# Last layer of a four-layer backbone: the high and low halves of 256 tokens read as one moving operand of 512 columns

## The chip, the core and the metric

The kernel runs on one core of a Trainium2 chip. TensorE (PE) multiplies, VectorE (DVE) and ScalarE (ACT) do the elementwise work, GpSimd (POOL) issues a few DMAs, SyncE (SP) issues most of them. The metric is the device time of one execution in microseconds; lower is better. Each engine works through its own queue in the order in which the program put it there, and waits at the head of the queue when an operand is not ready.

## What is computed

A latent stream of 256 tokens and a context stream of 256 tokens, each 1024 wide, pass through four layers. Each layer is a mixer and a squared-ReLU MLP, each ahead of it a normalisation with shift and scale, behind it a gated residual. In the last layer the context stream is not needed any more beyond the mixer's keys and values, so its output projection and its MLP run on 256 tokens only.

```python
def sq_relu_mlp(x, w1, w2):
    return jnp.square(jax.nn.relu(x @ w1)) @ w2
...
    h = h + ml[2][:, None] * yl
    xl = modulate(rmsnorm(h, norm_g[l, 1]), ml[3][:, None], ml[4][:, None])
    h = h + ml[5][:, None] * sq_relu_mlp(xl, mlp_w1[l], mlp_w2[l])
```

Here `x` is (256, 1024), `w1` is (1024, 4096), `w2` is (4096, 1024), all float32. The output is the latent stream after a last normalisation.

## The kernel before

Every large product is made in three matmuls, because operands are split into a rounded high part (type fp32r) and the rest, a low part: high weight by high data, high weight by low data, low weight by high data (`mm3`, L388 to L392). Data lie transposed: 128 features on the partitions, tokens along the free axis, so that `xh` and `xl` hold for each of 8 feature chunks the 512 token columns, latent tokens in columns 0 to 255 (`LT`), context tokens behind them (`CT`).

A *chunk* is one packed weight tile of 128 x 1024: 8 blocks of 128 x 128, one for each step k over 1024 inputs. `chunk` (L404) fetches the weights, takes the next of six PSUM banks, issues 8 x 3 matmuls into it and then the evacuation of the bank. In layers 0 to 2 a matmul has 512 moving columns; in the last layer's output projection (L799) and MLP (L692 to L699) it has 256.

The order of the work around a chunk is that of the code, with nothing moved by a scheduler. `w_get` (L266) stands ahead of a chunk's matmuls and with `ahead=4` splits the weights that will be used four chunks later: ACT casts them to the high part `whi` (L241), DVE subtracts to get the low part `wlo` (L246), and then the DMA of another raw tile is issued. There are five pairs of `whi` and `wlo`, so the cast of a new one waits until PE has finished the chunk ahead of the present one. Behind the matmuls of the chunk come its evacuation's instructions, so that on ACT and DVE alike the order is: split for chunk m+4, evacuation of chunk m, split for chunk m+5, evacuation of chunk m+1, and so on.

The MLP runs in four blocks of hidden features. In each, a first half of 8 chunks makes 8 x 128 hidden features from `xh`, `xl` (evacuation `ev1`, L668), and a second half of 8 chunks multiplies these by `w2` and adds the result to `h` (`residual`, L558). The evacuation of a first-half chunk is on ACT: `r` = relu of the bank (L673), `hh` = its square rounded (L674), `q` = its square (L675); and on DVE `hl` = `q` - `hh` (L676). Step k of every chunk in the second half reads `hh`, `hl` of hidden chunk k, so the first chunk of the second half comes at its last step to the hidden chunk that was evacuated last. The evacuation of a second-half chunk is one DVE instruction (L565): `h` = bank x gate + `h`. The first three hidden chunks of an MLP are made inside `transition` (L577), behind the normalisation, and go through `ev1` too.

After the last block of the MLP, and in the last output projection, `stats_late` (L436) adds squares of `h` for the next normalisation.

Of the kernel before, what the change touches and what calls it, by code (L numbers as in the profile page):

```python
# [8 lines left out]
F32 = mybir.dt.float32  # L9
F32R = mybir.dt.float32r  # L10
# [3 lines left out]
ALU = mybir.AluOpType  # L14
# [8 lines left out]
NK = 8  # L23
# [10 lines left out]
HID_RING = 10  # L34
# [95 lines left out]
def ada_order():  # L130

    return [(l, cc) for l in range(DEPTH) for cc in range(0 if l else PE_ADA, 48)]
# [71 lines left out]
CT, LT, ALL = slice(T, 2 * T), slice(0, T), slice(0, 2 * T)  # L204
# [3 lines left out]
class Body:  # L208
# [185 lines left out]
    def unit(self, out, w, xk, sl, ks=range(NK)):  # L394

        for k in ks:
            hi, lo = xk(k)
            c = slice(k * 128, k * 128 + 128)
            self.mm3(out, w[0][:, c], w[1][:, c], hi[:, sl], lo[:, sl], k == 0, k == NK - 1)

    def x_chunk(self, k):
        return self.xh[:, k, :], self.xl[:, k, :]

# [154 lines left out]
    def residual(self, l, gate, stats):  # L558
# [14 lines left out]

        return evac


    def transition(self, tail, norm, n_head, evac_head, both):  # L577

# [82 lines left out]
    def mlp(self, l, last):  # L661
        nc = self.nc
        full = LT if last else ALL
        with ExitStack() as st:
            p1 = self.block_pool(st, f"mlp{l}", "right")
            hid = [(p1.tile([128, 512], F32R, name=f"hh{j}"), p1.tile([128, 512], F32R, name=f"hl{j}")) for j in range(4)]

            def ev1(ci, o, sl):  # L668
                n = sl.stop - sl.start
                hh, hl = hid[ci % HID_RING]  # L670
                r = p1.tile([128, 512], F32, tag="r", name="r", bufs=2)
                q = p1.tile([128, 512], F32, tag="q", name="q", bufs=1)
                nc.scalar.activation(r[:, :n], o, AF.Relu)  # L673
                nc.scalar.activation(hh[:, sl], r[:, :n], AF.Square)  # L674
                nc.scalar.activation(q[:, :n], r[:, :n], AF.Square)  # L675
                nc.vector.tensor_tensor(out=hl[:, sl], in0=q[:, :n], in1=hh[:, sl].bitcast(F32), op=ALU.subtract)  # L676

            yield 3, ev1
            p2 = self.block_pool(st, f"mlpb{l}", "right")
            hid += [(p2.tile([128, 512], F32R, name=f"hh{j}"), p2.tile([128, 512], F32R, name=f"hl{j}")) for j in range(4, HID_RING)]  # L680
            step = [0]
            if not last:
                p3_ctx = self.tc.tile_pool(name=f"mlpc{l}", bufs=1, side="right", reuse_waits="tile")
                p3 = p3_ctx.__enter__()
                self.conditions(p3)

            def pump():
                step[0] += 1
                if not last and step[0] > 2:
                    self.ada_pump(2 if step[0] % 6 else 1, l + 1)  # L690

            for b in range(4):  # L692
                for m in range(3 if b == 0 else 0, 8):
                    self.chunk(b * 8 + m, self.x_chunk, full, ev1)
                    pump()
                src = lambda k, b=b: hid[(b * 8 + k) % HID_RING]
                res = self.residual(l, 40, full.stop if b == 3 else 0)
                for m in range(5 if b == 3 and not last else 8):
                    self.chunk(m, src, full, res)  # L699
                    if b < 3 or m < 3:  # L700
                        pump()
            if not last:
                p3_ctx.__exit__(None, None, None)
            yield None if last else (src, res, (5, 6, 7))


    def mixer_a(self, l, i, last):
        nc, tc = self.nc, self.tc
        full = LT if last else ALL
        n = full.stop  # L710
        units = mixer_a_units()
        with ExitStack() as st:
# [38 lines left out]
            for u in range(n_head, len(units)):  # L751
                if units[u][0] == "gate":
                    w = self.w_get()
                    o = self.bank()
# [16 lines left out]
            for nh in range(2):  # L771
                outs = [self.bank() for _ in range(4)]
                for kk in range(4):
                    w = self.w_get()
# [11 lines left out]
                for tcn in range(4):  # L786
                    dst = vx[:, tcn, nh * 4 : nh * 4 + 4, 0:128]
                    src = outs[tcn].rearrange("p (h v) -> p h v", h=4)
# [8 lines left out]
            self.scan(l, i, last, sp, lp or sp, dnm, dar, qT, kT, vx, tok, saved, n)  # L797
        res = self.residual(l, 16, n)
        for m in range(3, 8 if last else 5):  # L799
            self.chunk(m, self.x_chunk, full, res, ahead=2 if last else 4)  # L800
        yield None if last else (self.x_chunk, res, (5, 6, 7))

    def gates(self, rows, dr, i, gps, last):
# [838 lines left out]
    def run(self):  # L1642
        nc = self.nc
        self.order = weight_order()
        self.ada_list = ada_order()
        self.n_ada = PE_ADA + len(self.ada_list)
        self.lows = []
        self.raw, self.hl, self.ada_raw, self.mods, self.rs, self.cur = {}, {}, {}, {}, {}, {}
        self.wpos = self.wsplit = self.apos = self.bpos = self.xpos = 0
        nc.scalar.preload_act_table_set("natural_log_exp_and_others")  # L1650
        cst = self.pool("cst", 1)
        big = self.pool("big", 1)
        self.modp = self.pool("mod", 2)
        self.nrm = self.pool("nrm", 1)
        self.adap = self.pool("ada", N_ADA)
        self.rawp = self.pool("raw", N_RAW)
        self.hlp = self.pool("hl", N_HL)
        self.dram = self.pool("dram", 1, space=DRAM)
        psum = self.pool("psum", 1, space=PSUM)
        self.allb = psum.tile([128, 8, 512], F32, name="bank")  # L1660
        self.banks = [self.allb[:, j, :] for j in range(8)]

        self.vecs = cst.tile([128, NV], F32, name="vecs")
        cons = self.cons = cst.tile([128, NC], F32, name="cons")
        self.cs = cst.tile([128, 8, 32], F32, name="cs")
        self.hgn = cst.tile([128, 16], F32, name="hgn")
        sk = cst.tile([128, 16], F32, name="sk")
        nc.sync.dma_start(out=self.vecs, in_=self.vecs_in)
        self.held = None
        self.sel = cst.tile([128, 2], F32, name="sel")  # L1670
        nc.gpsimd.dma_start(out=self.sel, in_=self.consts_in[:, CC["sel"] : CC["sel"] + 2])
        self.h = big.tile([128, 8, 512], F32, name="h")
        self.xh = big.tile([128, 8, 512], F32R, name="xh")
        self.xl = big.tile([128, 8, 512], F32R, name="xl")
        self.sq = cst.tile([128, 512], F32, name="sq")
        self.ssum = cst.tile([128, 512], F32, name="ssum")

        def con(name, w, rows=128):
            return cons[0:rows, CC[name] : CC[name] + w]

        self.ident, self.rot = con("ident", 128), con("rot", 128)
        self.cos, self.sin = con("cos", T), con("sin", T)
        self.mask_f, self.mask_b = con("mask_f", 128), con("mask_b", 128)
        self.ones = cst.tile([128, 128], F32, name="ones")
        nc.vector.memset(self.ones, 1.0)
        self.ones_row = self.ones
        self.eps = cst.tile([128, 1], F32, name="eps")
        nc.vector.memset(self.eps, EPS)
        nc.gpsimd.dma_start(out=sk, in_=self.sinks_in.to_broadcast([128, 16]))
        self.nsinks = cst.tile([128, 16], F32, name="nsinks")  # L1690
        self.ident16 = cst.tile([128, 128], BF16, name="ident16")
        self.mask_w = cst.tile([128, 2 * T], BF16, name="mask_w")

        def mixer(l):
            kind, i = l % 3, l // 3
            if kind == 0:
                return self.mixer_a(l, i, l == DEPTH - 1)
            return self.mixer_b(l, i) if kind == 1 else self.mixer_c(l, i)

        prev = mixer(0)  # L1700
        _, evac = next(prev)
        self.start(5, evac)
        nc.vector.tensor_scalar(self.hgn, self.vecs[:, VC["a_head_g"] : VC["a_head_g"] + 16], -1.0, None, op0=ALU.mult)
        nc.vector.tensor_scalar(self.nsinks, sk, -1.0, None, op0=ALU.mult)
        tail = prev.send(5)
        for b in range(1, 2 * DEPTH):
            l, which = divmod(b, 2)
            block = self.mlp(l, l == DEPTH - 1) if which else mixer(l)
            n_head, evac = next(block)
            self.transition(tail, (l, which), n_head, evac, tail is not None)  # L1710
            next(prev, None)
            prev = block
            tail = next(block)
        step = self.rstd_begin(0, self.stats_mm(0, more=self.sq_late))
        for c in range(NK - 2, NK):
            self.scale_out(c)
        step()
        for c in range(0, NK, 2):
            hc = self.h[:, c : c + 2, LT]
            self.nc.vector.tensor_tensor(out=hc, in0=hc, in1=self.rs[0].unsqueeze(1).to_broadcast([128, 2, T]), op=ALU.mult)  # L1720
            (self.nc.sync, self.nc.scalar)[c // 2 % 2].dma_start(out=self.out[:, c : c + 2, :], in_=hc)
        next(prev, None)
# [29 lines left out]
```

## Time and profile before

| | us |
|---|---|
| median of 3 runs | 2112.53 (2112.12 to 2112.61) |
| profiled execution, its own time | 2114.74 |
| its span, from first to last instruction | 2113.0 |
| PE busy | 2053.4 (97%) |
| DVE busy | 1453.5 (69%) |
| ACT busy | 948.9 (45%) |
| last layer's MLP, first chunk behind `transition` to its last matmul | 1925.34 to 2101.2 |

A row of a timeline gives the start, the duration, the engine, the line of the kernel, the operation, its operands and, in brackets, how long the engine was idle before it and what released it. The end of a matmul is modelled, since matmuls are pipelined; the distance between the starts of two of them is what one costs. The granted clock of TensorE (`PEclk`) is 1.00 at 2.4 GHz and 0.50 at 1.2 GHz; a value between is a stretch that holds both.

### The profile page before, as it was taken

To read this page: it belongs to the slowest core of one execution; us is meant where nothing else is said; L and a number is where in the kernel's file an instruction comes from. 1 tells how busy PE (TensorE), PEld (TensorE's weight loads), DVE (VectorE), ACT (ScalarE), POOL (GpSimd) and SP (SyncE) were. 2 spreads that over 40 slices of the span, in tenths; PEclk is the share of its full clock that TensorE was granted. 3 is DMA by queue.
4 is the path that set the end of the run, shared out by engine and by line. 5 is a ranking of instruction groups with operands and counts; after the bars stand their busy time and mean duration, and the time that the engine had idled before them with its cause. 6 is when DMAs were issued, how large, how long until landed. Compare 5 with 4: busy or idle time off the path is not lost.

```text
span 2113.0 us, 30325 instructions
## 1 busy us (share of the span) xinstructions
PE 2053.4 (97%) x11730; PEld 1751.2 (83%) x11730; DVE 1453.5 (69%) x2652; ACT 948.9 (45%) x1814; POOL 87.0 (4%) x138
## 2 busy tenths in 40 slices
PE   6989999999999999999999999999999999989998
PEld 4767798888889878988888988898888899889997
DVE  5667777787777775677777764467777776576554
ACT  3436653324236685624333343262433435556554
POOL 0123100000000000000000000000000000310000
PEclk9999999999999999999999999999999999999999
DMA  9783245565553104266565433236556533635552
GB/s 300 272 264 103 64 135 179 177 193 185 184 170 119 50 2 138 92 189 189 179 194 175 130 112 98 94 108 189 187 180 197 179 122 104 175 103 180 184 185 91
DMA packets 97025, 326.11 MB, mean 154 GB/s; under 512 B 17760, under 2 KB 18928, under 8 KB 96240
## 3 DMA queue, kind: packets, MB, share of 16 engines
q1 hardware_dynamic: 81184, 293.81, 43.5%
q0 software_dynamic: 15152, 29.83, 4.6%
q8 instruction: 92, 1.51, 0.3%
q10 hardware_dynamic: 544, 0.52, 0.1%
q14 instruction: 53, 0.43, 0.1%
HBM read 319.73 MB, written 4.33 MB: 153 GB/s over the span
## 4 chain that ended last, share of the span: by engine, by line
PE 92%; DVE 3%; DMA 2%; ACT 2%; issue 1%; POOL 0%; SPq 0%; DVEq 0%; ACTq 0%
PE bank L390 25%; PE bank L392 25%; PE bank L391 25%; PE bank L591 2%; PE bank L592 2%; PE bank L594 2%; PE bank L422 1%; PE bank L1348 1%; PE bank L423 1%; PE bank L424 1%; PE bank L1360 1%; DMA ab<-dar 1%; PE bank L1288 1%; PE bank L1025 1%; DVE wlo L246 1%; PE bank L1000 1%
## 5 line engine op out<-in xcount | busy, mean ns | idle before, releaser
L390 PE MATMUL bank<-xh,whi 128*128 128x512 f32 (+1 forms) x1600 | 579.4, 362 | 1.7 <-ACT h L912 1.0
L241 ACT CAST whi<-raw 128x1024 fp32r<-128x1024 f32 x374 | 387.1, 1044 | 421.1 <-PE bank L391 382.8
L391 PE MATMUL bank<-xl,whi 128*128 128x512 f32 (+1 forms) x1600 | 574.4, 359 | 0.2
L392 PE MATMUL bank<-xh,wlo 128*128 128x512 f32 (+1 forms) x1600 | 573.9, 359 | 0.0
L246 DVE TENSOR_TENSOR wlo<-raw,whi 128x1024 fp32r<-128x1024 f32 x374 | 455.6, 1225 | 152.5 <-ACT whi L241 151.9
L353 DVE SCALAR_TENSOR_TENSOR junk<-ada,cbc 128x1024 bf16<-128x1024 f32 x320 | 390.7, 1221 | 18.1 <-DMA ada<-in_ada 13.8
L390 PE MATMUL bank<-hh,whi 128*128 128x512 f32 (+1 forms) x1096 | 384.5, 351 | 0.0
L392 PE MATMUL bank<-hh,wlo 128*128 128x512 f32 (+1 forms) x1096 | 383.9, 350 | 0.0
L391 PE MATMUL bank<-hl,whi 128*128 128x512 f32 (+1 forms) x1096 | 383.9, 350 | 0.0
L390 PEld LDWEIGHTS bank<-xh,whi 128*128 128x128 f32 x1600 | 304.9, 191 | 49.9 <-ACT h L912 1.6
L392 PEld LDWEIGHTS bank<-xh,wlo 128*128 128x128 f32 x1600 | 304.9, 191 | 44.3
L391 PEld LDWEIGHTS bank<-xl,whi 128*128 128x128 f32 x1600 | 305.0, 191 | 44.0 <-DVE xl L945 1.0
L391 PEld LDWEIGHTS bank<-hl,whi 128*128 128x128 f32 x1096 | 207.4, 189 | 27.4
L392 PEld LDWEIGHTS bank<-hh,wlo 128*128 128x128 f32 x1096 | 207.4, 189 | 27.2
L390 PEld LDWEIGHTS bank<-hh,whi 128*128 128x128 f32 x1096 | 207.4, 189 | 27.1
L565 DVE SCALAR_TENSOR_TENSOR h<-bank,mod,h 128x256 f32<-128x256 f32 x280 | 125.6, 479 | 133.1 <-PE bank L392 133.1
L676 DVE TENSOR_TENSOR hl<-q,hh 128x512 fp32r<-128x512 f32 (+1 forms) x137 | 81.5, 595 | 170.5 <-ACT q L675 170.2
L673 ACT ACTIVATE r<-bank 128x512 f32<-128x512 f32 (+1 forms) x137 | 70.8, 517 | 269.2 <-PE bank L392 266.2
L459 ACT ACTIVATE sq<-h 128x256 f32<-128x256 f32 (+1 forms) x74 | 36.0, 487 | 139.4 <-DVE h L565 114.2
L591 PE MATMUL bank<-xh,whi 128*128 128x256 f32 x312 | 81.4, 289 | 3.5 <-ACT xh L527 3.5
L592 PE MATMUL bank<-xh,wlo 128*128 128x256 f32 x312 | 80.2, 285 | 0.0
L674 ACT ACTIVATE hh<-r 128x512 fp32r<-128x512 f32 (+1 forms) x137 | 75.9, 554 | 4.6
(274 smaller groups left out, 2129.3 us busy)
## 6 DMA issues: line engine op xcount, KB each, us to landing
raw<-in_wts SPq DMA_DIRECT2D x374, 512.0 KB, 4.2
ada<-in_ada SPq DMA_DIRECT2D x160, 512.0 KB, 3.5
start<-in_ada SPq DMA_DIRECT2D x16, 512.0 KB, 9.1
first<-in_ada POOLq DMA_DIRECT2D x12, 512.0 KB, 6.0
cbc<-line POOLq DMA_DIRECT2D x4, 1024.0 KB, 7.8
rb<-dnm POOLq DMA_DIRECT2D x16, 256.0 KB, 7.1
ab<-dar POOLq DMA_DIRECT2D x16, 256.0 KB, 12.2
h<-in_hin SPq DMA_DIRECT2D x4, 512.0 KB, 6.8
```

What stands on the lines that cost most here:

```text
L241: self.nc.scalar.copy(hi, self.raw[j])
L246: self.nc.vector.tensor_tensor(out=lo, in0=self.raw.pop(j), in1=hi.bitcast(F32), op=ALU.subtract)
L353: nc.vector.scalar_tensor_tensor(out=junk, in0=w, scalar=1.0, in1=self.cbc[:, s, :], op0=ALU.mult, op1=ALU.mult, accum_out=self.mods[l][:, ...
L390: mm(out, lhsT=whi, rhs=xhi, start=first, stop=False)
L391: mm(out, lhsT=whi, rhs=xlo, start=False, stop=False)
L392: mm(out, lhsT=wlo, rhs=xhi, start=False, stop=last)
L565: self.nc.vector.scalar_tensor_tensor(out=self.h[:, m, a:b], in0=o[:, a - sl.start : b - sl.start], scalar=mod[:, gate + m, s : s + 1], in ...
L591: mm(o[:, :T], lhsT=w[0][:, c], rhs=hi[:, sl], start=(k == 0), stop=False)
L592: mm(o[:, :T], lhsT=w[1][:, c], rhs=hi[:, sl], start=False, stop=False)
L673: nc.scalar.activation(r[:, :n], o, AF.Relu)
L674: nc.scalar.activation(hh[:, sl], r[:, :n], AF.Square)
L676: nc.vector.tensor_tensor(out=hl[:, sl], in0=q[:, :n], in1=hh[:, sl].bitcast(F32), op=ALU.subtract)
```

## The change

`xh` and `xl` become the two halves of one tile `x2`, and each pair `hh`, `hl` the two halves of one tile `hh` (in the order's rows the low half then carries the name `hh` or `x2` as well). In the last layer a step k of a chunk is two matmuls instead of three: the high weight by 512 columns, 256 of the high data and 256 of the low data, into the two halves of a bank; and the low weight by the 256 high columns, added into the first half. The two halves of the bank are then added in the evacuation. This holds for the 5 chunks of the output projection that `chunk` handled and the 61 of the MLP; `transition`'s three keep the old form.

The new evacuation of a first-half chunk (`ev2`) is: ACT copies the second half of the bank to `a`; DVE adds the first half to it; DVE makes `q` = max(a, 0) x a; ACT rounds `q` to `hh`; DVE subtracts to get `hl`. That of a residual chunk (`residual2`) is the old instruction twice, once for each half of the bank.

```diff
+    def unit2(self, o, w, xk2, ks=range(NK)):
+        mm = self.nc.tensor.matmul
+        for k in ks:
+            x2 = xk2(k)
+            c = slice(k * 128, k * 128 + 128)
+            mm(o, lhsT=w[0][:, c], rhs=x2[:, :, LT], start=(k == 0), stop=(k == NK - 1))
+            mm(o[:, 0, :], lhsT=w[1][:, c], rhs=x2[:, 0, LT], start=False, stop=(k == NK - 1), skip_group_check=True)
+
+    def chunk2(self, m, xk2, evac2, ahead=4):
+        w = self.w_get(ahead)
+        o = self.bank().rearrange("p (s t) -> p s t", s=2)
+        self.unit2(o, w, xk2)
+        evac2(m, o)
...
+    def residual2(self, l, gate, stats):
...
+            for a in range(2):
+                self.nc.vector.scalar_tensor_tensor(
+                    out=self.h[:, m, LT], in0=o[:, a, :], scalar=mod[:, gate + m, 0:1], in1=self.h[:, m, LT],
+                    op0=ALU.mult, op1=ALU.add,
+                )
+            if stats:
+                self.stats_late(m, gate == 40)
...
+            def ev2(ci, o):
+                hh, hl = hid[ci % HID_RING]
+                r = p1.tile([128, 512], F32, tag="r", name="r", bufs=2)
+                a, q = r[:, LT], r[:, CT]
+                nc.scalar.copy(a, o[:, 1, :])
+                nc.vector.tensor_tensor(out=a, in0=o[:, 0, :], in1=a, op=ALU.add)
+                nc.vector.scalar_tensor_tensor(out=q, in0=a, scalar=0.0, in1=a, op0=ALU.max, op1=ALU.mult)
+                nc.scalar.copy(hh[:, LT], q)
+                nc.vector.tensor_tensor(out=hl[:, LT], in0=q, in1=hh[:, LT].bitcast(F32), op=ALU.subtract)
...
-                    self.chunk(b * 8 + m, self.x_chunk, full, ev1)
+                    if last:
+                        self.chunk2(b * 8 + m, self.x_chunk2, ev2)
...
-                    self.chunk(m, src, full, res)
+                    if last:
+                        self.chunk2(m, src2, res2)
...
-            self.chunk(m, self.x_chunk, full, res, ahead=2 if last else 4)
+            if last:
+                self.chunk2(m, self.x_chunk2, self.residual2(l, 16, True), ahead=2)
...
-        self.xh = big.tile([128, 8, 512], F32R, name="xh")
-        self.xl = big.tile([128, 8, 512], F32R, name="xl")
+        self.x2 = big.tile([128, 2, 8, 512], F32R, name="x2")
+        self.xh, self.xl = self.x2[:, 0], self.x2[:, 1]
```

PE, a second-half chunk of the MLP's last block, before (`whi`, `wlo` are the split weights, `hh`, `hl` the hidden features):

```order
L390 MATMUL bank<-hh_16365,whi_18262 128x256
L391 MATMUL bank<-hl_16366,whi_18262 128x256
L392 MATMUL bank<-hh_16365,wlo_18263 128x256
L390 MATMUL bank<-hh_16367,whi_18262 128x256
L391 MATMUL bank<-hl_16368,whi_18262 128x256
L392 MATMUL bank<-hh_16367,wlo_18263 128x256
```

and after:

```order
L407 MATMUL bank<-hh_16292,whi_17765 128x512
L408 MATMUL bank<-hh_16292,wlo_17766 128x256
L407 MATMUL bank<-hh_16293,whi_17765 128x512
L408 MATMUL bank<-hh_16293,wlo_17766 128x256
L407 MATMUL bank<-hh_16294,whi_17765 128x512
L408 MATMUL bank<-hh_16294,wlo_17766 128x256
```

Two matmuls stand for three, with the same 768 columns; 528 matmuls fewer in all. Ahead of the last layer's output projection PE's queue is the same, row for row.

DVE, the last first-half chunks of the MLP's third block and the first chunk of its second half, before:

```order
L246 TENSOR_TENSOR wlo_17564<-raw_17423,whi_17563 128x1024 [waits DVE_49,DMAHW2_49,PE_49,Activation_49]
L676 TENSOR_TENSOR hl_16201<-q,hh_16200 128x256 [waits Activation_49]
L246 TENSOR_TENSOR wlo_17600<-raw_17459,whi_17599 128x1024 [waits DVE_49,DMAHW3_49,PE_49,Activation_49]
L676 TENSOR_TENSOR hl_16203<-q,hh_16202 128x256 [waits Activation_49]
L246 TENSOR_TENSOR wlo_17636<-raw_17495,whi_17635 128x1024 [waits DVE_49,DMAHW4_49,PE_49,Activation_49]
L565 SCALAR_TENSOR_TENSOR h<-bank,mod_12109,h 128x256 [waits PE_49]
```

and after:

```order
L246 TENSOR_TENSOR wlo_17252<-raw_17143,whi_17251 128x1024 [waits DMAHW3_49,Activation_49]
L718 TENSOR_TENSOR r<-bank,r 128x256 [waits Activation_49]
L719 SCALAR_TENSOR_TENSOR r<-r 128x256 [waits DVE_49]
L721 TENSOR_TENSOR hh_16133<-r,hh_16133 128x256 [waits Activation_49]
L246 TENSOR_TENSOR wlo_17280<-raw_17171,whi_17279 128x1024 [waits DMAHW4_49,Activation_49]
L600 SCALAR_TENSOR_TENSOR h<-bank,mod_12078,h 128x256 [waits PE_49]
L600 SCALAR_TENSOR_TENSOR h<-bank,mod_12078,h 128x256 [waits DVE_49]
```

Between two weight subtractions stood one subtraction that waits for ACT; now three instructions stand there, two of which wait for ACT.

ACT, at first-half chunks of the same block, before:

```order
L673 ACTIVATE r<-bank 128x256
L674 ACTIVATE hh_16200<-r 128x256
L675 ACTIVATE q<-r 128x256
L241 CAST whi_17599<-raw_17459 128x1024
L673 ACTIVATE r<-bank 128x256
```

and after:

```order
L717 COPY r<-bank 128x256 [waits PE_49,Activation_49]
L720 CAST hh_16294<-r 128x256 [waits DVE_49]
L241 CAST whi_17167<-raw_17059 128x1024 [waits DMAHW0_49]
L717 COPY r<-bank 128x256 [waits PE_49,Activation_49]
L720 CAST hh_16130<-r 128x256 [waits DVE_49]
```

The cast of the next weights (L241) stood behind instructions that need the bank alone; it now stands behind one (L720) that waits for DVE.

## Rows read from the trace of the kernel before

**Rows 1.** Windows, block 1 of the last MLP: us, busy us (count) PE PEld DVE ACT POOL, clock, DMA.

```profile
1965.60:2011.70 46.10, 46.10 (x386) 46.10 (x386) 26.81 (x32) 24.76 (x40) 0.00 (x0) 1.00 0.58 184
```

**Rows 2.** Waits from 1925 to 2101: waiter, releaser, us in total, times, longest.

```profile
ACT whi L241 <- PE bank L391: 43.1, 27, 1.8
```

**Rows 3.** Timeline, one first-half chunk's end: start, us, engine, operation, [idle, releaser].

```profile
1965.66 0.28 PE L390 MATMUL bank<-xh,whi 128*128 128x256 f32 x1
1965.78 0.28 PE L391 MATMUL bank<-xl,whi 128*128 128x256 f32 x1
1965.86 0.38 ACT L673 ACTIVATE r<-bank 128x256 f32<-128x256 f32 x1 [1.95 <-PE bank L392]
...
1966.28 0.42 ACT L674 ACTIVATE hh<-r 128x256 fp32r<-128x256 f32 x1
...
1966.60 0.40 ACT L675 ACTIVATE q<-r 128x256 f32<-128x256 f32 x1
...
1966.91 1.04 ACT L241 CAST whi<-raw 128x1024 fp32r<-128x1024 f32 x1
...
1967.03 0.43 DVE L676 TENSOR_TENSOR hl<-q,hh 128x256 fp32r<-128x256 f32 x1 [1.87 <-ACT q L675]
...
1967.98 1.23 DVE L246 TENSOR_TENSOR wlo<-raw,whi 128x1024 fp32r<-128x1024 f32 x1 [0.52 <-ACT whi L241]
```

**Rows 4.** Timeline, matmuls of 512 columns in an earlier MLP, the tenth after the first.

```profile
1640.99 0.39 PE L392 MATMUL bank<-hh,wlo 128*128 128x512 f32 x1
...
1643.26 0.39 PE L390 MATMUL bank<-hh,whi 128*128 128x512 f32 x1
```

**Rows 5.** DVE in the timeline, and one row of the groups by form.

```profile
1899.69 1.22 DVE L246 TENSOR_TENSOR wlo<-raw,whi 128x1024 fp32r<-128x1024 f32 x1
1900.83 0.48 DVE L565 SCALAR_TENSOR_TENSOR h<-bank,mod,h 128x256 f32<-128x256 f32 x1
...
1913.12 0.42 DVE L495 SCALAR_TENSOR_TENSOR rs_a<-rs_a,rs_x 128x256 f32<-128x256 f32 x1
1913.58 0.42 DVE L496 SCALAR_TENSOR_TENSOR rs_y<-rs_a,rs_y 128x256 f32<-128x256 f32 x1
```

```profile
L1238 DVE TENSOR_TENSOR t<-bank,cons 128x256 f32<-128x256 f32 x10 | 4.2, 425 | 0.5
```

**Rows 6.** Chain that ended last, DVE handing to ACT: start, us, operation.

```profile
1914.04 0.50 DVE xt L524
1914.56 0.52 ACT xh L527
```

**Rows 7.** Timeline, first chunk behind `transition` in the last MLP.

```profile
1925.34 0.28 PE L390 MATMUL bank<-xh,whi 128*128 128x256 f32 x1
```

```profile
1929.53 3.50 DVE L246 TENSOR_TENSOR wlo<-raw,whi 128x1024 fp32r<-128x1024 f32 x3 [0.51 <-ACT whi L241]
...
1932.94 0.42 DVE L676 TENSOR_TENSOR hl<-q,hh 128x256 fp32r<-128x256 f32 x1
```

**Rows 8.** PE's waits from 1800 on, the windows behind some, and PE at the lower clock.

```profile
PE bank L972 <- DVE h L1088: 6.8, 2, 3.4
PE bank L591 <- ACT xh L527: 3.5, 1, 3.5
```

```profile
1850.00:1855.00 5.00, 3.76 (x18) 3.76 (x19) 3.76 (x11) 2.82 (x11) 0.54 (x2) 0.55 0.67 179
1855.00:1860.00 5.00, 5.00 (x45) 4.61 (x45) 2.32 (x9) 1.91 (x5) 1.22 (x3) 0.77 0.11 37
...
1915.00:1920.00 5.00, 4.88 (x28) 4.89 (x29) 4.90 (x13) 3.04 (x8) 0.00 (x0) 0.66 0.09 34
```

```profile
1915.51 0.42 PE L591 MATMUL bank<-xh,whi 128*128 128x256 f32 x1
...
1915.94 0.41 PE L591 MATMUL bank<-xh,whi 128*128 128x256 f32 x1
```

**Rows 9.** Timeline, the evacuation of the last chunk of all.

```profile
2101.22 0.48 DVE L565 SCALAR_TENSOR_TENSOR h<-bank,mod,h 128x256 f32<-128x256 f32 x1 [2.06 <-PE bank L392]
```

More of the change, by code (lines that the diff above doesn't have):

```diff
@@ L399, in unit, with x_chunk2 @@
             self.mm3(out, w[0][:, c], w[1][:, c], hi[:, sl], lo[:, sl], k == 0, k == NK - 1)
+    def unit2(self, o, w, xk2, ks=range(NK)):
[10 more added lines that the diff above has]
+        evac2(m, o)
+    def x_chunk2(self, k):
+        return self.x2[:, :, k, :]
     def x_chunk(self, k):
@@ L574, in residual, with evac @@
         return evac
+    def residual2(self, l, gate, stats):
+        mod = self.mods[l]
+        def evac(m, o):
+            for a in range(2):
[5 more added lines that the diff above has]
+                self.stats_late(m, gate == 40)
+        return evac
     def transition(self, tail, norm, n_head, evac_head, both):
@@ L665, in mlp @@
             p1 = self.block_pool(st, f"mlp{l}", "right")
-            hid = [(p1.tile([128, 512], F32R, name=f"hh{j}"), p1.tile([128, 512], F32R, name=f"hl{j}")) for j in range(4)]
+            hid2 = [p1.tile([128, 2, 512], F32R, name=f"hh{j}") for j in range(4)]
+            hid = [(t[:, 0], t[:, 1]) for t in hid2]
             def ev1(ci, o, sl):
@@ L676, in ev1 @@
                 nc.vector.tensor_tensor(out=hl[:, sl], in0=q[:, :n], in1=hh[:, sl].bitcast(F32), op=ALU.subtract)
+            def ev2(ci, o):
[7 more added lines that the diff above has]
+                nc.vector.tensor_tensor(out=hl[:, LT], in0=q, in1=hh[:, LT].bitcast(F32), op=ALU.subtract)
             yield 3, ev1
             p2 = self.block_pool(st, f"mlpb{l}", "right")
-            hid += [(p2.tile([128, 512], F32R, name=f"hh{j}"), p2.tile([128, 512], F32R, name=f"hl{j}")) for j in range(4, HID_RING)]
+            hid2 += [p2.tile([128, 2, 512], F32R, name=f"hh{j}") for j in range(4, HID_RING)]
+            hid += [(t[:, 0], t[:, 1]) for t in hid2[4:]]
             step = [0]
@@ L693, in mlp @@
                 for m in range(3 if b == 0 else 0, 8):
-                    self.chunk(b * 8 + m, self.x_chunk, full, ev1)
+                    if last:
+                        self.chunk2(b * 8 + m, self.x_chunk2, ev2)
+                    else:
+                        self.chunk(b * 8 + m, self.x_chunk, full, ev1)
                     pump()
                 src = lambda k, b=b: hid[(b * 8 + k) % HID_RING]
+                src2 = lambda k, b=b: hid2[(b * 8 + k) % HID_RING]
                 res = self.residual(l, 40, full.stop if b == 3 else 0)
+                res2 = self.residual2(l, 40, b == 3)
                 for m in range(5 if b == 3 and not last else 8):
-                    self.chunk(m, src, full, res)
+                    if last:
+                        self.chunk2(m, src2, res2)
+                    else:
+                        self.chunk(m, src, full, res)
                     if b < 3 or m < 3:
@@ L799, in mixer_a @@
         for m in range(3, 8 if last else 5):
-            self.chunk(m, self.x_chunk, full, res, ahead=2 if last else 4)
+            if last:
+                self.chunk2(m, self.x_chunk2, self.residual2(l, 16, True), ahead=2)
+            else:
+                self.chunk(m, self.x_chunk, full, res)
         yield None if last else (self.x_chunk, res, (5, 6, 7))
```

## The prediction

> **What bounds the kernel now.** I read the busy shares first, then the last layer's MLP by windows, then the waits, then the timeline of single chunks. In a block of the MLP (8 first-half and 8 second-half chunks, 46.1 us) PE and its weight loads are busy in every microsecond, DVE in 26.8, ACT in 24.8 [rows 1]. Who waits there are the others: ACT waits for PE to give back a pair of weight tiles, 43.1 us in 27 waits [rows 2]. So PE sets the time of this stretch, and the rest has slack; the question is what is left of it.
>
> **PE: what the merged matmul saves.** Two matmuls of 256 columns start 0.120 us apart [rows 3]; ten of 512 columns take 2.27 us, 0.227 each [rows 4]. The difference, 0.107, is 256 columns at 2.4 GHz; so each matmul has 0.013 us that doesn't depend on its columns, and the change removes one such share per step. A step goes from 3 x 0.120 = 0.360 to 0.227 + 0.120 = 0.347, a chunk of 8 steps from 2.88 to 2.776. With 66 chunks (5 in the output projection, 61 in the MLP), 528 steps: **-6.9 us** on PE. That the weights are loaded twice instead of three times per step is worth nothing beyond this: at either width the distance is columns plus the same share, so the loads are covered by the columns now.
>
> The Trainium skill, "TensorE: Matmul & The Clock Gate", Part 1 (the passage on 56 ns against 53.3), gives the share as about 2.5 ns per matmul. The rows show 13; by the page's figure the saving would be, as an estimate, 528 x 0.0025 = 1.3 us, and the sum below 5.6 higher. The measurement decides, so it gets no chance of its own.
>
> **The first half's evacuation becomes a loop between ACT and DVE.** Before, ACT's three instructions need only the bank, and nothing on ACT waits for DVE. After, the order on each engine is: DVE `wlo`(m+4), add, max-times, `hl`(m), `wlo`(m+5); ACT `whi`(m+4), copy, `hh`(m), `whi`(m+5). `hh`(m) waits for DVE's two instructions; the cast `whi`(m+5) is queued behind it; `wlo`(m+5) waits for the cast; and the add of chunk m+1 is queued behind `wlo`(m+5). That is a closed ring, once per chunk:
> - `wlo` to the add behind it: 1.14 (1900.83 - 1899.69) [rows 5];
> - add to max-times, which needs its result: 0.46, the distance of two dependent instructions of 256 columns [rows 5]; that the add reads a bank makes no difference in the nearest row, 425 ns [rows 5];
> - max-times to `hh` on ACT: 0.42 and a hand-over of 0.04 (0.52 behind an instruction of 0.48) [rows 6], 0.46;
> - `hh` to the cast behind it: 0.32 (1966.60 - 1966.28) [rows 3];
> - cast to `wlo`: 1.07 (1967.98 - 1966.91) [rows 3].
>
> Together **3.45 us per chunk** against PE's 2.776. No busy share shows this: DVE would do some 2.5 us of work per chunk and ACT 1.8. The evacuation falls 0.67 further behind PE with each first-half chunk.
>
> **Where that lands on PE.** The first second-half chunk reads hidden chunk 7 at its last step. Count from the end of a block's first chunk on PE. Blocks 1 to 3: ACT starts 0.20 later [rows 3], copy and hand-over 0.42, first add at 0.62. Eighth add at 0.62 + 7 x 3.45 = 24.77. Behind it max-times 0.46, `hh` 0.46, 0.42 + 0.03 to the subtraction, 0.43 + 0.05 for it: 1.85, so the hidden chunk is there at 26.62. PE wants it after seven more chunks and seven steps: 7 x 2.776 + 7 x 0.347 = 21.86. PE waits 4.76. (Before: 0.20 + 0.42 + 0.32 + 0.43 + 0.48 = 1.85 against 7 x 0.36 = 2.52; slack 0.7.)
>
> Block 0 has five such chunks, but begins late: behind `transition` three weight subtractions fill DVE from 1929.53, and the first evacuation's DVE step comes at 1932.94, 7.60 after PE began that chunk at 1925.34 [rows 7]. Before, this was harmless. Now the add stands in that place: 7.60 + 4 x 3.45 + 1.85 = 23.25, wanted at 5 x 2.776 + 2.43 = 16.31: PE waits 6.94. Sum: 6.94 + 3 x 4.76 = **+21.2 us**. In the second half the lag is gone: DVE has 1.14 + 0.52 + 0.40 = 2.1 us per chunk, ACT 1.04, no ring, so each block starts fresh. Banks (six) and split weights (four ahead) would only run out at a lag of more than four chunks.
>
> **TensorE's clock behind these waits.** From 1800 on PE waits three times for about 3.4 us [rows 8], and behind each stands a stretch at 1.2 GHz: granted clock 0.66 over 5 us (3.4 us at the lower level), or 0.55 and 0.77 (6.8 us) [rows 8]. There a matmul of 256 columns takes 0.215 ((1915.94 - 1915.51) / 2) [rows 8] instead of 0.120, so 3.4 us there lose 1.5. The second half that follows is PE's own, so this is paid in full. The four new waits are longer than those; I take 1.5 each, as behind the dense matmuls at 1915: **+6.0 us**. Bounds: 0.5 each (most of the low stretch lies in the wait itself) and 3.0 each (6.8 us), that is 2 to 12.
>
> **The residual twice.** In the second half the 32 additional DVE instructions hide in slack (2.1 of 2.78). The last chunk of the output projection and of the MLP have them on the path to the next normalisation: 0.48 [rows 9] and 0.04, twice, **+1.0**. The tile joined from `xh` and `xl` costs nothing: queues and waits ahead of the last layer are the same rows.
>
> **Sum.** -6.9 + 21.2 + 6.0 + 1.0 = +21.3 us. The profiled execution has a span of 2113.0 and a time of 2114.74, 1.74 outside, which I leave as it is; its time would be 2136.0. The median before is 2112.53, so **2133.8, say 2134**.
>
> Bounds of the ring: if the add and max-times followed each other and ACT at 0.40 (the distance without dependence) rather than 0.46, and the rest shrank by 0.05, it is 3.28: 1.2 less in each of blocks 1 to 3, 0.7 less in block 0, -4.3. If each of the five hand-overs took 0.05 more it is 3.70: +1.75 three times and +1.0, +6.3.
>
> **Rivals.**
> *The evacuation keeps pace, faster.* If the ring were under about 2.8 us, no wait of PE would be left beyond some tenths, and the kernel would gain 6.9 - 1.0: 2106.6. For it: DVE and ACT each have slack in busy time. Against: `wlo` and the cast alone are 1.14 + 1.07, and three dependent instructions would have to fit in 0.6. It decides at 2.8; I see 3.45. 0.05. The Trainium skill, "Trainium Kernel Development and Optimization", Best Practices, warns that tiling speeds up TensorE but not the evacuation of PSUM; it gives no price, and the rows speak for it.
> *PE waits, but the clock holds.* 2133.8 - 6.0 = 2127.8. Against: every wait of this length in the rows was followed by a low stretch. 0.12.
> *The change doesn't do what it says on PE.* The moving operand comes in two pieces, and no row shows such a one. If it costs what two matmuls do, 0.240, the 6.9 is not saved, PE's slack grows by 0.1 per chunk (the waits shrink by about 0.9 and 0.7 a block, 3.4), and the time is 2133.8 + 6.9 - 3.4 = 2137.3. 0.08.
> *Lags that partly cancel, or a ring cut short by something I overlook,* so that saving and waits balance: within 2108.3 and 2116.8. 0.03.
>
> **How the numbers follow.** Forecast 0.72, rivals 0.05, 0.12, 0.08, 0.03. The measurement can tell about 0.2%, 4.2 us, from no change. Faster 0.05; same 0.03; slower 0.92. The range takes the ring's and the clock's bounds, half each at a time: below 2127.8 less 3.8, 2124; above 2134 plus 6 for the clock plus 4 for the ring, 2144. It covers the second and third rival too.
>
> **What would show it.** In the first halves: DVE waiting for ACT at `hl` and `wlo`, starts of the adds about 3.45 apart (right), or 2.78 (wrong). PE waiting once per block at its first matmul of step 7 of the first second-half chunk, released by DVE's subtraction, about 7, 4.8, 4.8, 4.8 us; the granted clock below 1 behind each. Starts of a 512 and a 256 matmul 0.347 apart per step elsewhere. Wrong would be: no wait of PE between 1925 and 2101, or waits also in the second halves.

## The result and the profile after

| | before | after |
|---|---|---|
| median of 5 runs, us | 2112.12 (2111.27 to 2112.61) | 2136.64 (2135.14 to 2137.32) |
| ratio, 95% interval | | 1.0113 (1.0103 to 1.0124) |
| profiled execution, its own time | 2114.74 | 2136.74 |
| its span | 2113.0 | 2135.0 |
| last MLP, first chunk behind `transition` to last matmul | 175.6 | 198.1 |

The kernel became 24.5 us slower; forecast were 21.5, in a range of about 12 to 32. The spans differ by 22.0 only, because the profiled execution of before was 2.6 above this median and that of the changed kernel at its own. Of these 22.0, the last MLP has 22.5 (first chunk at 1924.45 instead of 1925.34, last matmul at 2122.50 instead of 2100.90), what lies behind it 0.4 more, and what lies ahead of it 0.9 less.

The windows of the MLP, cut where PE goes from first halves to second halves and back: stretch, length, then busy time and count of PE, PEld, DVE, ACT and POOL, granted clock, DMA. Of before:

```profile
1939.74:1962.78 23.04, 23.04 (x194) 23.04 (x193) 14.76 (x17) 9.44 (x12) 0.00 (x0) 1.00 0.69 212
1962.78:1985.82 23.04, 23.04 (x194) 23.04 (x193) 12.62 (x16) 15.39 (x29) 0.00 (x0) 1.00 0.57 176
```

and of after, all eight:

```profile
1924.45:1938.59 14.14, 14.14 (x83) 12.26 (x82) 9.16 (x14) 9.42 (x19) 0.00 (x0) 1.00 0.58 192
1938.59:1969.40 30.81, 24.87 (x130) 20.92 (x129) 22.69 (x34) 11.96 (x15) 0.00 (x0) 0.89 0.58 171
1969.40:1991.59 22.19, 22.19 (x131) 19.41 (x129) 15.29 (x26) 10.32 (x19) 0.00 (x0) 1.00 0.49 147
1991.59:2020.17 28.58, 24.30 (x131) 20.69 (x129) 21.28 (x31) 11.30 (x14) 0.00 (x0) 0.94 0.60 182
2020.17:2042.36 22.19, 22.19 (x131) 19.40 (x130) 15.29 (x26) 10.32 (x19) 0.00 (x0) 1.00 0.48 146
2042.36:2071.79 29.43, 25.14 (x130) 21.28 (x129) 21.26 (x31) 11.29 (x14) 0.00 (x0) 0.88 0.58 177
2071.79:2094.41 22.62, 22.62 (x130) 19.62 (x129) 15.49 (x26) 10.70 (x19) 0.00 (x0) 1.00 0.52 147
2094.41:2122.62 28.21, 24.36 (x130) 20.60 (x128) 17.57 (x30) 12.70 (x23) 0.00 (x0) 0.94 0.16 50
```

Read the lengths first. A first half of 8 chunks shrank from 23.04 to 22.19 or 22.62: PE gains. A second half grew from 23.04 to between 28.2 and 30.8, and its clock is below 1. Every microsecond lost lies in the second halves, although the evacuation that now goes back and forth between ACT and DVE (five instructions instead of four) is in the first. DVE's busy time in a first half is 15.3 of 22.2, and yet it is what PE will wait for.

Who waits (waiter, releaser, us in total, times, longest). Two more rows of before, beside the one in [rows 2], from 1925 to 2101:

```profile
DVE wlo L246 <- ACT whi L241: 26.0, 52, 0.7
DVE hl L676 <- ACT q L675: 24.5, 27, 2.7
```

and after, over the last layer:

```profile
ACT hh L720 <- DVE r L719: 48.1, 28, 2.2
ACT whi L241 <- PE bank L407: 44.2, 25, 3.5
...
PE bank L407 <- DVE hh L721: 18.4, 9, 2.8
DVE wlo L246 <- ACT whi L241: 17.7, 32, 1.5
DVE hh L721 <- ACT hh L720: 13.7, 29, 0.5
```

ACT still waits for PE to give back weight tiles, in the second halves. DVE waited for ACT before too, at the weights and at the subtraction. New is the other direction: ACT waits for DVE's max-times, and with that the waits close into a ring. And PE, which nobody held up in the MLP before, waits for DVE's subtraction. The ring itself, on DVE in block 1 (start, duration, operation, [idle, releaser]); L718 is the add, L719 max-times, L721 the subtraction:

```profile
1976.23 0.42 DVE L718 TENSOR_TENSOR r<-bank,r 128x256 f32<-128x256 f32 x1
1976.69 0.43 DVE L719 SCALAR_TENSOR_TENSOR r<-r 128x256 f32<-128x256 f32 x1
1977.59 0.42 DVE L721 TENSOR_TENSOR hh<-r,hh 128x256 fp32r<-128x256 f32 x1 [0.47 <-ACT hh L720]
1978.54 1.23 DVE L246 TENSOR_TENSOR wlo<-raw,whi 128x1024 fp32r<-128x1024 f32 x1 [0.53 <-ACT whi L241]
1979.68 0.42 DVE L718 TENSOR_TENSOR r<-bank,r 128x256 f32<-128x256 f32 x1
```

From add to add 3.45 us, the number that was put together from five rows of before. The two idle times in brackets, 0.47 and 0.53, are the ring: DVE waits for ACT's rounding and then for ACT's cast, which stands behind the rounding.

And PE where this lands, in block 1's first second-half chunk:

```profile
1993.55 0.28 PE L408 MATMUL bank<-hh,wlo 128*128 128x256 f32 x1
1995.30 0.50 PE L407 MATMUL bank<-hh,whi 128*128 128x512 f32 x1 [1.46 <-DVE hh L721]
1995.63 0.28 PE L408 MATMUL bank<-hh,wlo 128*128 128x256 f32 x1
1998.73 0.49 PE L407 MATMUL bank<-hh,whi 128*128 128x512 f32 x1 [2.82 <-DVE hh L721]
```

PE waits at step 6 for hidden chunk 6 and at step 7 for hidden chunk 7. (The idle time is counted from a modelled end; from the starts, step 7 begins at 1998.73 instead of 1991.59 + 7 x 0.347 = 1994.02, 4.71 late.)

### The profile page after: what moved, and what is told of

It reads as the page before. It is cut to its first block, busy times and chain, and to the rows that moved or that the text cites. A ratio compares the mean times of both kernels' runs of the same rounds, so it can differ in the third digit from the quotient of the medians.

```text
span 2135.0 us, 29330 instructions
## 1 busy us (share of the span) xinstructions
PE 2055.7 (96%) x11202; PEld 1725.3 (81%) x11202; DVE 1491.9 (70%) x2747; ACT 937.6 (44%) x1785; POOL 85.8 (4%) x138
## 5 line engine op out<-in xcount | busy, mean ns | idle before, releaser
L241 ACT CAST whi<-raw 128x1024 fp32r<-128x1024 f32 x374 | 387.5, 1045 | 421.3 <-PE bank L391 339.7
L390 PE MATMUL bank<-x,whi 128*128 128x512 f32 (+1 forms) x1328 | 501.6, 378 | 1.9 <-ACT h L969 1.2
L391 PE MATMUL bank<-x,whi 128*128 128x512 f32 (+1 forms) x1328 | 496.8, 374 | 0.2
L392 PE MATMUL bank<-x,wlo 128*128 128x512 f32 (+1 forms) x1328 | 496.3, 374 | 0.0
L390 PE MATMUL bank<-hh,whi 128*128 128x512 f32 (+1 forms) x840 | 312.0, 371 | 0.0
L392 PE MATMUL bank<-hh,wlo 128*128 128x512 f32 (+1 forms) x840 | 311.5, 371 | 0.0
L391 PE MATMUL bank<-hh,whi 128*128 128x512 f32 (+1 forms) x840 | 311.5, 371 | 0.0
L390 PEld LDWEIGHTS bank<-x,whi 128*128 128x128 f32 x1328 | 252.2, 190 | 50.2 <-ACT h L969 1.8
L391 PEld LDWEIGHTS bank<-x,whi 128*128 128x128 f32 x1328 | 252.4, 190 | 43.9 <-DVE x L1002 1.0
L392 PEld LDWEIGHTS bank<-x,wlo 128*128 128x128 f32 x1328 | 252.3, 190 | 43.9
L391 PEld LDWEIGHTS bank<-hh,whi 128*128 128x128 f32 x840 | 158.3, 188 | 27.4
L390 PEld LDWEIGHTS bank<-hh,whi 128*128 128x128 f32 x840 | 158.3, 188 | 27.3
L407 PE MATMUL bank<-hh,whi 128*128 128x512 f32 x256 | 97.5, 421 | 18.4 <-DVE hh L721 18.4
L407 PE MATMUL bank<-x,whi 128*128 128x512 f32 x272 | 95.5, 396 | 0.0
L624 PE MATMUL bank<-x,whi 128*128 128x256 f32 x312 | 81.6, 290 | 3.5 <-ACT x L545 3.5
```

Of the source, the lines that this page charges most:

```text
L241: self.nc.scalar.copy(hi, self.raw[j])
L390: mm(out, lhsT=whi, rhs=xhi, start=first, stop=False)
L391: mm(out, lhsT=whi, rhs=xlo, start=False, stop=False)
L392: mm(out, lhsT=wlo, rhs=xhi, start=False, stop=last)
L407: mm(o, lhsT=w[0][:, c], rhs=x2[:, :, LT], start=(k == 0), stop=(k == NK - 1))
L624: mm(o[:, :T], lhsT=w[0][:, c], rhs=hi[:, sl], start=(k == 0), stop=False)
```

## The experiments

All changes are against the changed kernel. On the two chips of the experiments single runs of the kernel before spread from 2107.9 to 2115.3. Much of such a spread lies ahead of the last layer: in the ten traces the last MLP's first chunk behind `transition` begins anywhere between 1917.2 and 1925.3. So beside each median stands the length of the last MLP in the trace, from the first chunk behind `transition` to the last matmul (before 175.6, changed 198.1). The main rival to the ring is that the added work, and not its order, is what costs; the first and the sixth experiment are aimed at it, the others at single terms of the sum.

**The cast ahead of the rounding.** The split of the next weights, ACT's cast and DVE's subtraction, moves ahead of the instructions that wait.

```diff
 nc.scalar.copy(a, o[:, 1, :])
+wlo = self.w_half() if ci % 8 < 7 else None
 nc.vector.tensor_tensor(out=a, in0=o[:, 0, :], in1=a, op=ALU.add)
 nc.vector.scalar_tensor_tensor(out=q, in0=a, scalar=0.0, in1=a, op0=ALU.max, op1=ALU.mult)
+if wlo:
+    wlo()
 nc.scalar.copy(hh[:, LT], q)
```

> The changed kernel with one order altered: in a first-half chunk the split of the next weights stands on ACT ahead of the rounding to hh, and on DVE ahead of the subtraction to hl (not at the eighth chunk of a half). The same instructions, so that the cast no longer waits for DVE's max-times. If the ring between ACT and DVE is the cause: DVE has add 0.46, max-times 0.36, wlo 1.14, subtraction 0.36 = 2.3 us per chunk, under PE's 2.776; no wait of PE in blocks 1 to 3 (some 0.05), and in block 0, whose evacuation starts 4.2 late, (7.60 + 4 x 2.4 + 1.85) - 16.31 = about 2.7, with up to 1.5 for the clock behind it. Time 2112.1 - 6.9 + 1.0 + 2.7 + 0 to 1.5 = 2109 to 2110.5. If instead the added work of the evacuation is the cause, or the matmul of two pieces, nothing changes: 2130 to 2137.

Measured: 2109.09 (ratio to before 0.9988, 0.9978 to 0.9997), MLP 173.5. The same instructions in another order took 24.6 us off the MLP. ACT in the timeline:

```profile
1967.06 0.37 ACT L717 COPY r<-bank 128x256 f32<-128x256 f32 x1 [1.10 <-PE bank L408]
1967.32 1.05 ACT L241 CAST whi<-raw 128x1024 fp32r<-128x1024 f32 x1
1968.38 0.41 ACT L723 CAST hh<-r 128x256 fp32r<-128x256 f32 x1
1969.83 0.37 ACT L717 COPY r<-bank 128x256 f32<-128x256 f32 x1 [1.04 <-PE bank L408]
```

ACT waits for PE again, once per chunk of 2.77, and not for DVE. PE's only wait in the MLP is 1.4 us in block 0 (1.9 from the starts, 2.7 expected):

```profile
PE bank L407 <- DVE hh L724: 1.4, 2, 1.1
```

No stretch at the lower clock followed it. So the ring is the cause, and the added work is not.

**Merged only where there is no ring.** The first halves go back to `chunk` and `ev1`.

```diff
-                    if last:
-                        self.chunk2(b * 8 + m, self.x_chunk2, ev2)
-                    else:
-                        self.chunk(b * 8 + m, self.x_chunk, full, ev1)
+                    self.chunk(b * 8 + m, self.x_chunk, full, ev1)
```

> Merged matmuls only in the second halves and the output projection, where no evacuation goes back and forth between ACT and DVE; the first halves as before. If a merged step saves 0.013 us and the doubled residual hides: 37 chunks x 8 x 0.013 = 3.9 less, 1.0 more on the two ends of chains: 2109.2, no wait of PE in the MLP. If a matmul's own share were 2.5 ns as a page has it, or if the 32 additional DVE instructions delayed weights or banks: 2112.4 or more.

Measured: 2108.85 (0.9987, 0.9977 to 0.9997), MLP 173.9, no wait of PE in it. The direction came out. The size of the whole did too (2.4 below before, 2.9 expected), but that is in part luck: in the MLP only 1.7 us instead of 3.3 were gained, with second halves of 22.61 instead of 8 x 2.776 = 22.2. A step takes 0.353 there, see below.

**The ring without the merged matmul.**

```diff
-            mm(o, lhsT=w[0][:, c], rhs=x2[:, :, LT], start=(k == 0), stop=(k == NK - 1))
+            for a in range(2):
+                mm(o[:, a, :], lhsT=w[0][:, c], rhs=x2[:, a, LT], start=(k == 0), stop=(k == NK - 1), skip_group_check=True)
```

Here the two halves of a bank are begun by matmuls of their own, and this kernel presumably leaves a part of step 0's product out of the sum (its output is off; no run shows the cause by itself). Number, shape and order of the instructions are those described, and only the time is read here.

> The changed kernel with the wide matmul taken apart again: high by high and high by low each 256 columns, into the two halves of the bank, evacuation as changed. It has the ring without PE's saving. By the ring: chunk 2.88, waits (23.25 - 16.92) + 3 x (26.62 - 22.68) = 18.2 instead of 21.2, PE 6.9 more, clock the same 7.9: 2136.6 + 6.9 - 3.0 = 2140.5. If the wide matmul in two pieces were itself what costs, this would be below the changed kernel's 2136.6.

Measured: 2137.84 (1.0125, 1.0110 to 1.0140), MLP 200.1, 2.1 longer than the changed kernel's. First halves are back at 23.04, and the second half behind them still waits, at a lower clock:

```profile
1967.48:1990.52 23.04, 23.04 (x194) 23.04 (x193) 15.51 (x27) 11.07 (x20) 0.00 (x0) 1.00 0.46 152
1990.52:2018.85 28.33, 25.56 (x194) 24.75 (x193) 21.00 (x30) 10.49 (x13) 0.00 (x0) 0.94 0.53 175
```

The matmul of two pieces isn't what costs. Expected were 3.9 more than the changed kernel, 6.9 for PE less 3.0 of waits; in the MLP 2.1 came. The steps away from the waits are 0.360 apart here, as before, so what the MLP is longer than before, 200.1 - 175.6 = 24.5, is waits and clock alone. In the changed kernel these are 28.2 (worked out in the next section), 3.7 more instead of 3.0, and the merged matmul gave back 28.2 - 22.5 = 5.7 in the MLP, where 61 chunks at 0.104 are 6.3.

**Work for PE inside the waits.** Matmuls into an unused bank ahead of steps 6 and 7.

```diff
...
+            self.unit2(o, w, xk2, range(6))
+            for k in (6, 7):
+                for _ in range(fill[k - 6]):
+                    self.nc.tensor.matmul(self.banks[7], lhsT=w[0][:, 0:128], rhs=self.xh[:, 0, :], start=True, stop=True)
+                self.unit2(o, w, xk2, range(k, k + 1))
...
```

> The changed kernel with matmuls of 512 columns into an unused bank ahead of steps 6 and 7 of each block's first second-half chunk: 12 and 12 in block 0, 6 and 12 in the others, 0.227 each at the full clock, to lie inside PE's waits. The hidden chunk comes no earlier. If the clock behind the waits costs what the trace shows (second halves 28.3 us longer than 8 chunks each, 20.4 of it waits, 7.9 the clock): granted clock 1.0 all through the MLP and 2136.6 - 7.9 = 2128.7. If the stretch behind the waits is long for another reason: 2136 or more.

Measured: 2127.45 (1.0076, 1.0061 to 1.0091), MLP 192.1. Second halves:

```profile
1931.31:1960.65 29.34, 28.94 (x155) 23.97 (x153) 22.51 (x34) 11.96 (x15) 0.00 (x0) 1.00 0.58 179
...
1983.26:2010.24 26.98, 26.98 (x149) 22.92 (x147) 20.90 (x30) 10.90 (x14) 0.00 (x0) 1.00 0.60 188
```

The granted clock is 1.00 in all of them. Block 1's second half is 26.98 instead of 28.58, the four together 110.3 instead of 117.0. The first halves are 0.8 longer in sum (22.61 three times, a pace of which more below), and the waits for the last hidden chunk are shorter by as much, 19.6 from the starts instead of 20.4. What lies behind the waits fell from 7.8 to 2.0, so the lower clock behind a wait is a cost of its own, here 5.8 us. By the MLP, which lost 5.9 us where 7.9 were expected, the time would be 2130.7; that the median lies even below the expected 2128.7 is luck.

**Block 0's late start.**

```diff
-                        self.chunk2(b * 8 + m, self.x_chunk2, ev2)
+                        self.chunk2(b * 8 + m, self.x_chunk2, ev2, ahead=4 if b else 2)
...
-                        self.chunk2(m, src2, res2)
+                        self.chunk2(m, src2, res2, ahead=3 if b == 0 and m == 0 else 4)
```

> The changed kernel, with the weights of block 0's first half split two chunks ahead instead of four, one split per chunk, so that three splits no longer stand ahead of the first evacuation. If block 0's longer wait comes from that late start: its first add comes 0.62 behind PE's first chunk, its last hidden chunk at 2.78 + 0.62 + 4 x 3.45 + 1.85 = 19.05 instead of 23.25, wanted at 16.31: a wait of 2.7 instead of 6.7 measured, blocks 1 to 3 unchanged. From the MLP's first chunk behind transition to its last matmul 194.0 us instead of 198.05, up to 2 less if the clock holds. If it comes from something else in transition: 198.

Measured: 2133.02 (1.0105, 1.0091 to 1.0118), MLP 194.4. The start of PE's last step in block 0's first second-half chunk:

```profile
1942.40 0.28 PE L408 MATMUL bank<-hh,wlo 128*128 128x256 f32 x1
1945.35 0.50 PE L407 MATMUL bank<-hh,whi 128*128 128x512 f32 x1 [2.66 <-DVE hh L721]
```

From the starts 2.83 more than a step's 0.12, where 2.74 were expected and the changed kernel had 6.7. That the two agree is luck, since two errors cancel. The first evacuation starts later than expected:

```profile
1929.70 0.42 DVE L718 TENSOR_TENSOR r<-bank,r 128x256 f32<-128x256 f32 x1
```

This is 5.34 behind PE's first chunk (at 1924.36), where 2.78 + 0.62 = 3.40 were expected and the changed kernel has 7.60. And PE comes to its last step later, because of two small waits for `wlo` (0.8 in all by the list, 1.6 from the starts), the price of the shorter lead. What the run does show is that block 0's end moves with its start: the first add comes 2.26 earlier, and step 7 begins 20.99 behind the first chunk instead of 23.25, again 2.26 earlier. Behind this shorter wait no low clock followed.

**One link more in the ring, and the same instruction outside it.**

```diff
 nc.vector.tensor_tensor(out=a, in0=o[:, 0, :], in1=a, op=ALU.add)
+nc.vector.scalar_tensor_tensor(out=a, in0=a, scalar=0.0, in1=a, op0=ALU.max, op1=ALU.max)
 nc.vector.scalar_tensor_tensor(out=q, in0=a, scalar=0.0, in1=a, op0=ALU.max, op1=ALU.mult)
```

> The changed kernel with one more DVE instruction of 256 columns in the ring: max first, then max-times. If the ring sets the lag: period 3.45 + 0.46 = 3.91, each of blocks 1 to 3 waits 8 x 0.46 = 3.7 longer, block 0 5 x 0.46 = 2.3: PE's waits from 20.4 to 33.8, the MLP from 198.0 to 211.4, plus or minus 2 for the clock. If only DVE's busy time counted (some 2.5 us per chunk, then 2.9 against PE's 2.776): at most 8 x 0.13 per block, some 4 more.

Measured: 2149.62 (1.0182, 1.0168 to 1.0196), MLP 212.1, 14.0 longer. DVE, from add to add 3.91:

```profile
1977.29 0.42 DVE L718 TENSOR_TENSOR r<-bank,r 128x256 f32<-128x256 f32 x1
...
1981.20 0.42 DVE L718 TENSOR_TENSOR r<-bank,r 128x256 f32<-128x256 f32 x1
```

29 instructions of 0.46 (13.3 us of DVE) cost 14.0 us of the MLP, the clock's part among them. The counterpart, in `residual2`:

```diff
+            if gate == 40 and m < 7:
+                hm = self.h[:, m, LT]
+                self.nc.vector.tensor_tensor(out=hm, in0=hm, in1=hm, op=ALU.max)
```

> The changed kernel with one more dependent DVE instruction of 256 columns behind the residual of 31 second-half chunks (all but the eighth of each block, the maximum of h with itself). The same instruction as one more in the first half, but in no ring. If only the ring matters: PE's waits and the MLP as in the changed kernel, 198 plus or minus 1. If DVE's total work in the MLP matters: about 28 x 0.46 = 13 more.

Measured: 2134.13 (1.0113, 1.0098 to 1.0129), MLP 198.6. The 28 additional instructions (seven in each block; the 31 of the expectation is a slip) cost 0.5 us, within what the low stretches vary by (here 6.8, 6.8, 3.4, 3.4 us). DVE in that stretch is nearly full, idle 0.17 per chunk, and PE doesn't wait for it:

```profile
1952.47 1.00 DVE L600 SCALAR_TENSOR_TENSOR h<-bank,mod,h 128x256 f32<-128x256 f32 x2 [0.17 <-PE bank L408]
1953.51 0.42 DVE L606 TENSOR_TENSOR h<-h 128x256 f32<-128x256 f32 x1
1953.85 1.22 DVE L246 TENSOR_TENSOR wlo<-raw,whi 128x1024 fp32r<-128x1024 f32 x1
```

The same instruction on the same engine costs next to nothing outside the ring, and its whole length in it.

**All of it together.** The cast ahead of the rounding, the early start, and the last chunk of the output projection and of the MLP in the old form:

```diff
+                        if b == 3 and m == 7:
+                            self.chunk(m, src, full, res)
...
-            if last:
+            if last and m < 7:
                 self.chunk2(m, self.x_chunk2, self.residual2(l, 16, True), ahead=2)
             else:
-                self.chunk(m, self.x_chunk, full, res)
+                self.chunk(m, self.x_chunk, full, res, ahead=2 if last else 4)
```

> The cast-first order with that early start, and the last chunk of the output projection and of the MLP in the old form, which takes the doubled residual off the two chains. No wait of PE in the MLP over 0.2. Steps at 0.347 to 0.353: MLP 175.56 - 61 x 8 x (0.0067 to 0.013) = 169.2 to 172.3 us; behind the last matmul 12.1 instead of 12.5. Against the kernel before 3.5 to 7 less: ratio 0.9967 to 0.9985. If merged matmuls had no gain of their own: 1.000.

Measured: 2108.45 against 2110.93 of before on the same chip, ratio 0.9986 (0.9978 to 0.9995); MLP 172.1, no wait of PE in it. It beats both kernels, by 0.14% over the one before, which is just outside the 0.15 to 0.33% that were expected; from the cast-first kernel and the one without first halves the times can't tell it apart (only the MLP's length does: 172.1, 173.5, 173.9). Two of its first halves:

```profile
1960.08:1982.27 22.19, 22.19 (x130) 19.59 (x129) 18.64 (x31) 13.16 (x22) 0.00 (x0) 1.00 0.63 193
...
2005.01:2027.63 22.62, 22.62 (x130) 19.62 (x129) 18.70 (x31) 13.15 (x22) 0.00 (x0) 1.00 0.58 185
```

## Why the prediction was right, step by step

| step | forecast, us | measured, us |
|---|---|---|
| period of the ring | 3.45 | 3.45 |
| waits of PE in blocks 0, 1, 2, 3 | 6.94, 4.76, 4.76, 4.76 | 6.7, 4.7, 4.7, 4.3 |
| their sum | 21.2 | 20.4 |
| lower clock behind them | 6.0 | 7.8, of which 5.8 went with the clock held |
| the residual twice, behind the MLP | 0.5 | 0.4 |
| merged matmuls, the MLP's 61 of 66 chunks | -6.3 of -6.9 | -5.7 |

- **The ring.** Put together from single rows ([rows 3, 5, 6]) it came out to 0.01 us, and with it the waits. They are the distance of step 7's start from the half's start, less 7 x 0.347 (block 0: 1947.70 - 1938.59 - 2.43); block 3's is shorter because its first half took 0.4 longer on PE. The row that the hand-over of 0.04 was read from has 0.50 and not 0.48, which would make that link 0.44; in the changed kernel it is 0.46, as taken. What the prediction didn't say is that PE stops twice in that chunk, at step 6 and at step 7 (in block 0 at step 5 too); the sum is the same, because the last hidden chunk ends it.
- **Block 0's start.** Taken from one row, the time at which DVE reached the subtraction [rows 7]; the changed kernel's first add came 7.60 behind the first chunk, as taken, and the early-start run shows that block 0's end moves with this start one for one.
- **The clock.** All four waits had a low stretch behind them, as forecast. The four second halves are 117.0 us long, 28.2 more than 32 chunks of 2.776; 20.4 of that are waits, 7.8 remain: 1.9, 1.7, 2.5 and 1.7 in blocks 0 to 3, where the sum took 1.5 for each. That is the largest miss of the sum, within its bounds of 2 to 12. Most of it are steps that begin 0.64 apart instead of 0.347, five to seven behind each wait; of block 1:

```profile
2001.48 0.63 PE L407 MATMUL bank<-hh,whi 128*128 128x512 f32 x1
2001.90 0.41 PE L408 MATMUL bank<-hh,wlo 128*128 128x256 f32 x1
2002.12 0.63 PE L407 MATMUL bank<-hh,whi 128*128 128x512 f32 x1
```

Two of the low stretches were of some 6.8 us and two of 3.4, where the sum took 3.4 for all; but the long ones began inside the wait (in block 0 the granted clock is 0.62 from 1944.0 to 1947.6, and step 7 begins at 1947.70), so they cost little more than the short ones. The filling matmuls show that it is the clock and not something else behind a wait: of the 2.0 that were left with them, 1.5 are the slower pace of the next point.

- **The merged matmul saved less, most of all where nothing waits.** A step was to take 0.347. It does in some stretches (22.19 for 64 steps) and takes 0.353 in others (22.62), so the saving per step is 0.013 or 0.007. Of the changed kernel's eight stretches five, away from waits and low clock, have the faster pace, and the MLP's saving is 5.7 instead of 6.3. Of the best kernel's eight, with no wait left, two have it; it has gained 3.5 us in the MLP over 480 merged steps, 0.0073 each, where 6.2 were to be expected. The 2.5 ns per matmul of the Trainium skill, "TensorE: Matmul & The Clock Gate", Part 1, which the prediction weighed, lie below both; the measurement decides.
- **The rivals.** That the evacuation keeps pace fell with the first trace, and came true, but for a wait of 1.9 in block 0, once the weight split was moved: 2109.1, against 2106.6 worked out for it. That the clock holds was met in the filled kernel only: 2127.5, against 2127.8, closer than its MLP bears out. That the merged matmul saves nothing on PE fell with the 22.19 of a first half, against 23.04 before.

The forecast of 2134 is 2.6 below the median. The terms account for 0.7 of it, the spans' 22.0 instead of 21.3: the clock 1.8 more, PE's saving in the MLP 0.6 less, the waits 0.8 shorter, and 0.9 less ahead of the MLP, which no term forecast. The rest is chiefly the base: the profiled execution of before is 2.2 above the median that the forecast started from, and that of the changed kernel is at its median.

## What to carry to other kernels

A busy share says nothing of an engine that hands work to and fro: follow the instructions of one round through both queues, with everything that stands in line behind a waiting one, and compare the length of that ring with the time in which the bottleneck makes one round. Here DVE was busy for 69% of a first half and still fell 0.67 us behind with each chunk, and moving one independent weight split, a cast on ACT and a subtraction on DVE, ahead of the instructions that wait (no work saved, no buffer added) took the MLP from 198.1 to 173.5 us. Look for the bill where the last result is read, not where the work was added, and add the lower clock behind it, here 1.7 to 2.5 us behind each wait of 4.3 to 6.7.

## What the runs showed of the hardware that was not expected

- The pair of a 512-column and a 256-column matmul has two paces at the same granted clock of 1.00: 0.347 or 0.353 per step, kept for whole first halves. In the best kernel a first half over the same operands takes 22.19 once and 22.62 twice; in the kernel with filled waits every full first half takes 22.61. The pace changes behind a wait of PE in some traces. What sets it was not found; it is worth about 3 us of this kernel.
- Waits of 2.8 us (early start, block 0) and 1.9 us (cast first, block 0) were followed by no lower clock; the four of 4.3 to 6.7 us in the changed kernel all were, though single steps of PE break them (in block 1: 1.46, a step, 2.82).
